# A decoder block's MLP: a written order of engines where the phases meet, first loads into early buffers, and two of four product sums per pair made by TensorE on copied banks

## The chip, the cores and the metric

The kernel runs on one core of a Trainium2 chip. The metric is the device time of one execution in microseconds (us), shown as the median of several runs. One further execution is recorded by the hardware profiler; its instruction times are the source of the rows below. PE is TensorE, DVE VectorE, ACT ScalarE, POOL GpSimd, SP SyncE (here it issues DMAs); PEld is PE's weight load.

## The reference

One layer over 1024 tokens of 1024 features in float32: a mixer half (pooling heads and state-space heads with one input and one output projection) and then an MLP half. Each half is normalised and is shifted, scaled and gated by vectors that come from a condition `c`. The change concerns the MLP half:

```python
u = rms_norm(h, g_mlp[layer]) * (1.0 + scale_f) + shift_f
f = jnp.square(jax.nn.relu(jnp.einsum('bsd,df->bsf', u, w_up[layer])))     # 1024 -> 4096
h = h + gate_f * jnp.einsum('bsf,fd->bsd', f, w_down[layer])               # 4096 -> 1024
return rms_norm(h, g_final)
```

Ahead of it stand the mixer's steps: `u = rms_norm(h) * (1 + scale_m) + shift_m`, the projection by `w_in`, windowed means, a causal convolution with silu, a chunked state-space scan, a grouped norm, and `h = h + gate_m * (y_mix @ w_out)`.

## The kernel before

**Precision.** TensorE multiplies a shortened float32 form. Each float32 operand is split into `hi` (a cast, on ACT) and `lo` (operand minus `hi`, on DVE); a product is three matmuls, hi by hi, hi by lo, lo by hi (`mm3`, line 244). So every operand needs one ACT cast and then one DVE subtraction before TensorE can use it, and PE waits for the cast and, two matmuls on, for the subtraction.

**Up-projection by seven products.** Tokens and features are halved, so u has four blocks (A11, A12 for the first 512 tokens, A21, A22 for the second), each of four 128 x 512 slices. `w_up` is taken in 16 pairs m of two 128-column groups, with blocks B11, B12, B21, B22. A Strassen-like scheme needs seven block products a pair instead of eight. Its left operands, made once, are named in `ORDER`: A11, S1 = A21 - A22, A12, E6 = S1 - A11, G3 = E6 + A12, A22, E7 = A11 - A21. Its right operands are sums of weight blocks, made per pair in `wx` or in place and split into `whl` tiles by `prep_up(m, j)`. Product j of a pair is written (m, j); a product is 4 x 3 = 12 matmuls of 512 columns. Products share PSUM banks: `KEYS` names bank a, b, c or d of the pair. `after_up(m, j)` takes results out of the banks, forms the four outputs by additions on DVE, applies squared relu (`act2`, on DVE) and writes seven combinations to DRAM (`f_d`) for the down-projection, a seven-product scheme too.

**The two meetings.** After the output projection the tokens' rows are normalised (`norm_xn`, rows `xn`), turned by PE (`turn_xn`, four 128-column transposes a bank) and scaled and shifted into u (`affine`). The first half of the tokens is done during the output projection; the second half after it. While it is made PE does six *early* products, (m, 0) and (m, 2) for the first three pairs (`NA = 3`), whose weights come from the pool of the projection's `raw`, `hi` and `lo` units. That pool is closed before the pool for the raw weights of whole pairs (`wraw`, 1 MB a load) is opened. The second meeting is that of up and down. A unit g of the down stage needs `fr` (from `f_d`) and, in the first eight units, `xs` (from `w_down`), 512 KB each (`load_dn`), and four tiles `dhi`, `dlo` in the pool `fp` (`prep_dn`). `LD = 3` units are loaded ahead and `LP = 2` are split ahead. The residual rows `hres` are read back into `tok`, whose space holds the up stage's intermediate values (`F`) until then.

**Order.** Engines run their instructions strictly in the order of their own queues. That order comes from a scheduler, except inside `pinned(...)`, where the named engines keep the written order. A tile of a pool waits until the tile that held its slot before is no longer used; the pool `fp` has 12 slots, `actp` 16.

Of the kernel before, what the change touches and what calls it, by code (L numbers as in the profile page):

```python
# [9 lines left out]
F32 = mybir.dt.float32  # L10
# [59 lines left out]
def tile_hybrid_block(  # L70
# [218 lines left out]
    um = ExitStack()  # L289
    unitm = enter(um, name="unitm", bufs=1, side="right")  # L290
    accp = enter(um, name="accp", bufs=1, side="right")
# [690 lines left out]
    F = [tok[:, 4 * i:4 * i + 4, :].rearrange("p t (a c) -> p (t a) c", c=HW) for i in range(2)]  # L982
    xn_ = {}
# [34 lines left out]

    def u2_h0(k):
# [3 lines left out]
        v = F[0][:, k, :]  # L1023
        affine(act if k % 2 == 0 else dve, v, px, k)
        dve.tensor_tensor(out=s_[:, 1, :], in0=v, in1=s_[:, 0, :].bitcast(F32), op=ALU.subtract)
        U["A11" if k < 4 else "A12"][k % 4] = s_
# [15 lines left out]
    for m in range(NA):  # L1042
        for i in range(2):
# [22 lines left out]

    ORDER = ("A11", "S1", "A12", "E6", "G3", "A22", "E7")
    MID = ("B11", "U1", "B21", "T2", "B22", "T4", "T3")
    banks, snap, wraw, wx, hl = {}, {}, {}, {}, {}

    def mm_up(m, j, w, key, first):
        b_ = banks[m, key] = bank() if first else banks[m, key]
        for k in range(4):
            a = U[ORDER[j]][k]
            whi, wlo = w[k]
            mm3(b_, whi, wlo, (a[:, 0, :], a[:, 1, :]), first and k == 0, k == 3)

    KEYS = ("a", "b", "c", "a", "b", "d", "a")
    FIRST = (True, True, True, False, False, True, False)
    LAST = (False, False, True, False, True, True, True)  # L1080
    early = [(m, i, get(1, 2)[0:4]) for m in range(NA) for i in range(2)]
    um.close()
    upst = ExitStack()
    wp = enter(upst, name="wup", bufs=1, side="right")

    def load_up(m):
        wraw[m] = wp.tile([P, KD, 2 * P], F32, name="wraw", tag="wraw", bufs=2)
# [8 lines left out]
    def prep_up(m, j):  # L1096
        r = wraw[m]
        b11, b12, b21, b22 = r[:, 0:4, 0:P], r[:, 0:4, P:2 * P], r[:, 4:8, 0:P], r[:, 4:8, P:2 * P]
        if j == 1:
            wx[m] = wp.tile([P, 4, P], F32, name="wx", tag="wx", bufs=2)  # L1100
# [8 lines left out]
        t_ = wp.tile([P, 2, 4, P], F32R, name="whl", tag="whl", bufs=4)  # L1109
        act.copy(t_[:, 0], src)  # L1110
        dve.tensor_tensor(out=t_[:, 1], in0=src, in1=t_[:, 0].bitcast(F32), op=ALU.subtract)  # L1111
        hl[m, j] = [(t_[:, 0, k, :], t_[:, 1, k, :]) for k in range(4)]

    def act2(v):
        dve.scalar_tensor_tensor(out=v, in0=v, scalar=0.0, in1=v, op0=ALU.max, op1=ALU.mult)  # L1115


    def after_up(m, j):
        f = F[m % 2]
        if j == 0:  # L1120
            s1 = f[:, 0, :]
            if m < NA:
                s1 = snap[m] = wp.tile([P, HW], F32, name="snap", tag="snap", bufs=NA)
            act.copy(s1, banks[m, "a"])
        elif j == 1:
            act.copy(f[:, 5, :], banks[m, "b"])
        elif j == 2:
            add(f[:, 0, :], banks[m, "c"], snap.get(m, f[:, 0, :]))
            act2(f[:, 0, :])
        elif j == 3:  # L1130
            act.copy(f[:, 2, :], banks[m, "a"])
        elif j == 4:
            sub(f[:, 2, :], banks[m, "b"], f[:, 2, :])
            act2(f[:, 2, :])
        elif j == 6:
            act.copy(f[:, 7, :], banks[m, "a"])  # L1136
# [10 lines left out]
    def mm_up(m, j, w):  # L1147
        key = KEYS[j]
        if FIRST[j]:
            banks[m, key] = bank()  # L1150
        for k in range(4):
            a = U[ORDER[j]][k]
            whi, wlo = w[k]
            mm3(banks[m, key], whi, wlo, (a[:, 0, :], a[:, 1, :]), FIRST[j] and k == 0, k == 3, more=not (FIRST[j] and LAST[j]))

    for n_, (m, i, w) in enumerate(early):
        mm_up(m, 2 * i, w)
        if i == 0:
            after_up(m, 0)
        r = n_ - 2 * NA + 4  # L1160
        if r >= 0:
            for k in (r, r + 4):
                affine(act, F[1][:, k, :], turn_xn(1, k), k)
    load_up(0)
    load_up(1)
    s1f = [fp.tile([P, 2, HW], F32, name="s1f", tag="a") for _ in range(2)]
    prep_up(0, 1)
    for k in range(4):
        v = s1f[k // 2][:, k % 2, :]
        sub(v, F[1][:, k, :], F[1][:, 4 + k, :])  # L1170
        U["S1"][k] = split(actp, v, "S1")
    prep_up(1, 1)
    for m in range(2):
        mm_up(m, 1, hl.pop((m, 1)))
    for k in range(4):
        v = s1f[k // 2][:, k % 2, :]
        sub(F[1][:, k, :], F[0][:, k, :], F[1][:, k, :])
        sub(F[0][:, k, :], v, F[0][:, k, :])
        U["E6"][k] = split(actp, F[0][:, k, :], "E6")
    prep_up(0, 3)  # L1180
    prep_up(1, 3)
    for m in range(2):
        mm_up(m, 3, hl.pop((m, 3)))
    for k in range(4):
        add(F[0][:, 4 + k, :], F[0][:, k, :], F[0][:, 4 + k, :])
        U["G3"][k] = split(fp, F[0][:, 4 + k, :], "G3")
    prep_up(0, 4)
    prep_up(1, 4)
    after_up(0, 2)
    after_up(0, 1)  # L1190
    after_up(0, 3)
# [240 lines left out]
```

## Time and profile before

| | |
|---|---|
| median of 3 runs (lowest to highest) | 1201.95 us (1201.36 to 1202.45) |
| profiled execution, its own time | 1201.51 us |
| its span, first to last instruction | 1199.8 us |
| mean granted TensorE clock | 0.983 |
| busy PE, DVE, ACT | 1153.1, 880.7, 520.4 us |
| end of the first meeting's transposes | 563.5 us |
| up stage at a steady pace | from about 613 us |
| first down matmul | 882.13 us |

Rows of a timeline read: start in us, length in us, engine, line, operation, output <- inputs, form, count, and in brackets the idle time of the engine before the row and who ended it. A row with a count covers consecutive instructions of one form, and its length reaches to the end of the last, whose tail overlaps the next instruction. Rows by stage give the stretch and its length, then for each engine busy us (count), then the granted clock, the DMA engines' busy share, and GB/s.

### The profile page before, as it was taken

What the parts mean: (1) busy time and instruction counts of PE and PEld (TensorE: products, weight loads), DVE (VectorE), ACT (ScalarE), POOL (GpSimd) and SP (SyncE); (2) the same over time, 40 slices, a digit from 0 to 9 for tenths busy, and PEclk for the clock granted to TensorE, in tenths of its full rate; (3) what the DMA queues carried; (4) which work ended last, traced back from release to release, by engine and by line L of the source; (5) the groups of instructions that cost most, each with busy time, mean ns of one, the idle gap of its engine ahead of it and who ended that gap; (6) DMA issues with size and microseconds to landing.
All of it is one profiled execution on the core that took longest, in us unless ns stands there. A gap on an engine that the chain in (4) does not pass through costs nothing. (4 is left out here: it accounts for less than half of the span.)

```text
span 1199.8 us, 15415 instructions
## 1 busy us (share of the span) xinstructions
PE 1153.1 (96%) x5569; PEld 950.0 (79%) x5569; DVE 880.7 (73%) x1313; ACT 520.4 (43%) x913; POOL 184.6 (15%) x208
## 2 busy tenths in 40 slices
PE   6889999999999999997989999999979999999997
PEld 5678787787899888886768888888868888888885
DVE  6978889967978646747897867777648744577984
ACT  4266575544443624527433333332324444334363
POOL 4234446515400012022000000000000000000030
PEclk9989999999999999999989999999989999999999
DMA  9831243223277637734145353444598844776732
GB/s 294 236 90 51 70 128 107 71 87 129 81 231 224 209 103 240 244 97 141 57 179 185 120 170 141 148 150 140 208 346 295 299 123 123 232 230 239 263 123 88
DMA packets 125644, 200.73 MB, mean 167 GB/s; under 512 B 8416, under 2 KB 67584, under 8 KB 123520
## 3 DMA queue, kind: packets, MB, share of 16 engines
q1 hardware_dynamic: 125072, 199.39, 50.4%
q8 instruction: 43, 0.70, 0.2%
q14 instruction: 33, 0.27, 0.1%
q10 hardware_dynamic: 240, 0.30, 0.1%
q0 software_dynamic: 256, 0.07, 0.1%
HBM read 159.81 MB, written 39.91 MB: 166 GB/s over the span
## 5 line engine op out<-in xcount | busy, mean ns | idle before, releaser
L244 PE MATMUL bank<-u,hi 128*128 128x512 f32 x560 | 186.3, 414 | 2.1 <-ACT u L252 2.0
L244 PE MATMUL bank<-dhi 128*128 128x512 f32 (+1 forms) x452 | 175.6, 390 | 7.2 <-ACT dhi L1277 6.1
L244 PE MATMUL bank<-dlo,dhi 128*128 128x512 f32 (+1 forms) x452 | 176.2, 390 | 0.6 <-DVE dlo L1278 0.6
L244 PE MATMUL bank<-dhi,dlo 128*128 128x512 f32 (+1 forms) x452 | 175.9, 389 | 0.0
L179 POOL TENSOR_TENSOR rst<-ssq,mhalf 128x1 f32<-128x1 f32 (+2 forms) x27 | 27.3, 1013 | 721.5 <-DVE ssq L178 696.4
L244 PEld LDWEIGHTS bank<-u,hi 128*128 128x128 f32 x560 | 105.3, 192 | 30.5 <-issue 5.0
L1278 DVE TENSOR_TENSOR dlo<-fr,dhi 128x1024 fp32r<-128x1024 f32 x56 | 68.5, 1222 | 81.8 <-ACT dhi L1277 81.8
L1277 ACT CAST dhi<-fr 128x1024 fp32r<-128x1024 f32 x56 | 58.6, 1047 | 155.9 <-PE bank L244 117.4
L244 PE MATMUL bank<-hi,ym 128*128 128x512 f32 x384 | 125.6, 400 | 0.0
L244 PE MATMUL bank<-u,lo 128*128 128x512 f32 x280 | 111.4, 398 | 0.0
L194 ACT CAST hi<-raw 128x512 fp32r<-128x512 f32 (+2 forms) x109 | 67.7, 631 | 87.4 <-PE bank L244 66.8
L244 PEld LDWEIGHTS bank<-dhi 128*128 128x128 f32 x452 | 85.4, 189 | 25.3 <-ACT dhi L1277 6.5
L244 PEld LDWEIGHTS bank<-dlo,dhi 128*128 128x128 f32 x452 | 85.5, 189 | 18.8 <-DVE dlo L1278 1.3
L195 DVE TENSOR_TENSOR lo<-raw,hi 128x512 fp32r<-128x512 f32 (+1 forms) x87 | 64.9, 756 | 47.8 <-ACT hi L194 46.7
L244 PEld LDWEIGHTS bank<-dhi,dlo 128*128 128x128 f32 x452 | 85.6, 189 | 17.6
L244 PE MATMUL bank<-hi,u 128*128 128x256 f32 (+1 forms) x512 | 97.7, 289 | 0.1
L244 PE MATMUL bank<-E,whl 128*128 128x512 f32 x384 | 94.8, 396 | 0.0
L244 PEld LDWEIGHTS bank<-E,whl 128*128 128x128 f32 x384 | 72.6, 189 | 17.5
L244 PEld LDWEIGHTS bank<-hi,ym 128*128 128x128 f32 x384 | 72.1, 188 | 16.2 <-issue 0.5
L244 PEld LDWEIGHTS bank<-hi,u 128*128 128x128 f32 x512 | 80.7, 190 | 1.3 <-issue 0.7
L244 PE MATMUL bank<-u,whl 128*128 128x512 f32 x312 | 77.0, 396 | 0.0
L244 PE MATMUL bank<-lo,ym 128*128 128x512 f32 x192 | 75.4, 393 | 0.0
(249 smaller groups left out, 2168.1 us busy)
## 6 DMA issues: line engine op xcount, KB each, us to landing
f_d<-tok SPq DMA_DIRECT2D x16, 1792.0 KB, 6.7
fr<-f_d SPq DMA_DIRECT2D x56, 512.0 KB, 4.1
wr<-in_w_down_dram SPq DMA_DIRECT2D x56, 512.0 KB, 5.1
raw<-in_w_ada_dram SPq DMA_DIRECT2D x64, 256.0 KB, 3.2
wraw<-in_w_up_dram SPq DMA_DIRECT2D x16, 1024.0 KB, 7.2
raw<-in_w_in_dram SPq DMA_DIRECT2D x48, 256.0 KB, 2.9
raw<-in_w_out_dram SPq DMA_DIRECT2D x48, 256.0 KB, 2.8
tok<-in_x_dram SPq DMA_DIRECT2D x16, 512.0 KB, 6.3
```

The costliest lines, as they stand in the source:

```text
L179: pool.tensor_tensor(out=rst[:, a:b], in0=m, in1=mhalf[:, :b - a], op=ALU.pow)
L194: act.copy(hi[:, :n], raw[:, :n])
L195: (pool if ring.get("pool_lo") else dve).tensor_tensor(out=lo[:, :n], in0=raw[:, :n], in1=hi[:, :n].bitcast(F32), op=ALU.subtract)
L244: pe.matmul(ps, lhsT=st_, rhs=mv, start=first and i == 0, stop=last and i == 2, skip_group_check=more)
L1277: act.copy(hi, src)
L1278: dve.tensor_tensor(out=lo, in0=src, in1=hi.bitcast(F32), op=ALU.subtract)
```

## The change

1. Left operands. S1 is made directly: ACT scales the turned A22 slice with a bias of the two shifts' difference (`dsh`), DVE scales the turned A21 slice and subtracts it, so S1 needs no separate u values. The shift is added to A22 later, in place on ACT. E6, G3, E7 and A22 are formed and split two slices at a time (1024 columns, `two`, `hi2`, `lo2`). `LONG` and `SHORT` name the slots of `F` where slices that live longer or shorter stand.
2. Order. The early units are all A11 first and A12 after. Then one `pinned` block writes ACT's, DVE's and PE's order from the first early product to (1, 5): three A11 products, the transposes and the S1 slices between the A12 products, S products for pairs 0 to 2, and so on. `prep_up` is split into `prep_hi` and `prep_lo`. From pair 4 on products run in the order 0, 1, 3, 2, 6, 4, 5.
3. Buffers. Pair 0's `wraw` and some `whl` tiles come from a new pool on the other side (`wupl`, every third pair) or from `lp`, so that they need not wait for the unit pool. The first three units' `fr` and all `xs` go to `actp`, and the first three units' loads are issued by POOL's queue during pair 15, with the first two `prep_dn` between pair 15's products.
4. Sums. `onward` copies bank a to a new bank on ACT (after product 0 to c, after 6 to d), and products 2 and 5 accumulate on the copy, in place of two DVE additions a pair. Relu and square of these two outputs move to ACT. The transposes clear a bank's accumulate state only with the first of four.

The diff's core:

```diff
     def turn_xn(h, k):
         px = bank()
         for i in range(4):
-            turn(px[:, i * P:(i + 1) * P], xn_[4 * h + i][:, k * P:(k + 1) * P])
+            pe.matmul(px[:, i * P:(i + 1) * P], lhsT=xn_[4 * h + i][:, k * P:(k + 1) * P], rhs=ident,
+                      is_transpose=True, start=i == 0, stop=i == 3, skip_group_check=True)
...
+    early = [get(1, 2)[0:4] for _ in range(2 * NA)]
+    am.close()
+    wlst = ExitStack()
+    wl = enter(wlst, name="wupl", bufs=1)
...
     def load_up(m):
-        wraw[m] = wp.tile([P, KD, 2 * P], F32, name="wraw", tag="wraw", bufs=2)
+        wraw[m] = (upp["r"] if m % 3 else wl).tile([P, KD, 2 * P], F32, name="wraw", tag="wraw", bufs=2 if m % 3 else 1)
...
+    def act2_bank(v, b_):
+        act.activation(out=v, in_=b_, func=AF.Relu)
+        act.activation(out=v, in_=v, func=AF.Square)
...
+    def onward(m, key):
+        banks[m, key] = bank()
+        act.copy(banks[m, key], banks[m, "a"])
...
     def after_up(m, j):
         f = F[m % 2]
         if j == 0:
-            s1 = f[:, 0, :]
-            if m < NA:
-                s1 = snap[m] = wp.tile([P, HW], F32, name="snap", tag="snap", bufs=NA)
-            act.copy(s1, banks[m, "a"])
+            onward(m, "c")
...
         elif j == 2:
-            add(f[:, 0, :], banks[m, "c"], snap.get(m, f[:, 0, :]))
-            act2(f[:, 0, :])
+            act2_bank(f[:, 0, :], banks[m, "c"])
...
         elif j == 6:
-            act.copy(f[:, 7, :], banks[m, "a"])
-            sub(f[:, 5, :], f[:, 5, :], f[:, 7, :])
-            add(f[:, 7, :], banks[m, "d"], f[:, 7, :])
-            act2(f[:, 5, :])
-            act2(f[:, 7, :])
+            onward(m, "d")
+            sub(f[:, 5, :], f[:, 5, :], banks[m, "a"])
+            (act2 if m > 1 else act2_on_act)(f[:, 5, :])
+        else:
+            act2_bank(f[:, 7, :], banks[m, "d"])
...
+    load_up(0)
+    with pinned((act, dve, pe)):
+        for m in range(NA):
+            mm_up(m, 0, early[m])
+            if m == 0:
+                prep_up(0, 1)
+        for m in range(NA):
+            after_up(m, 0)
         for k in range(4):
...
+            px = turn_xn(1, k + 4)
+            v = F[1][:, LONG[k], :]
+            act.activation(out=v, in_=px, func=AF.Identity, scale=sc_f[:, k + 4:k + 5], bias=dsh[:, k:k + 1])
+            px = turn_xn(1, k)
+            o = F[1][:, SHORT[k], :]
+            dve.scalar_tensor_tensor(out=o, in0=px, scalar=sc_f[:, k:k + 1], in1=v, op0=ALU.mult, op1=ALU.subtract)
+            s_ = actp.tile([P, 2, HW], F32R, name="S1", tag="a")
+            act.copy(s_[:, 0, :], o)
+            sub(s_[:, 1, :], o, s_[:, 0, :].bitcast(F32))
+            U["S1"][k] = (s_[:, 0, :], s_[:, 1, :])
+            if k < 3:
+                mm_up(k, 2, early[NA + k])
...
     def load_dn(g):
         p, u = units[g]
-        fr[g] = dp.tile([P, 2, HW], F32, name="fr", tag="fr", bufs=4)
-        sp.dma_start(out=fr[g], in_=f_d[u][:, :, PROD[p], :])
+        if g < LD:
+            fr[g] = actp.tile([P, 2, HW], F32, name="fr0", tag="a")
+        else:
+            fr[g] = dpp["d"].tile([P, 2, HW], F32, name="fr", tag="fr", bufs=4)
+        q = pool if g < LD else sp
+        q.dma_start(out=fr[g], in_=f_d[u][:, :, PROD[p], :])
...
+        if m == 15:
+            if j == 3:
+                for g in range(LD):
+                    load_dn(g)
+            elif j in (6, 4):
+                prep_dn(j == 4)
```

What this does to the queues, at the places where PE waits. First, DVE where the second half of u is made, before the change. (`s1f`, `S`, `G`, `E`: left operands and their lo parts; `wx` and `whl`: weight sum and its lo part.)

```order
L1094 TENSOR_TENSOR s1f<-tok 128x512
L1014 TENSOR_TENSOR G_5799<-tok,G_5799 128x512
L1094 TENSOR_TENSOR tok<-tok 128x512
L1014 TENSOR_TENSOR S_5704<-s1f,S_5704 128x512
L1091 TENSOR_TENSOR wx<-wraw 128x512
L1014 TENSOR_TENSOR E_5740<-tok,E_5740 128x512
L1014 TENSOR_TENSOR E_5745<-tok,E_5745 128x512
L1111 TENSOR_TENSOR whl<-wx,whl 128x512
```

And DVE at the same place after the change:

```order
L1101 TENSOR_TENSOR wx<-wraw 128x512
L178 TENSOR_SCALAR ssq<-ssq 128x1
L1141 TENSOR_TENSOR whl<-wx,whl 128x512
L1211 SCALAR_TENSOR_TENSOR tok<-bank,sc_f,tok 128x512
L1104 TENSOR_TENSOR S_5613<-tok,S_5613 128x512
...
L1104 TENSOR_TENSOR S_5694<-tok,S_5694 128x512
L1101 TENSOR_TENSOR wx<-wraw 128x512
L1104 TENSOR_TENSOR tok<-tok 128x2x512
L1141 TENSOR_TENSOR whl<-wx,whl 128x512
```

The first pair's weight sum and its split moved ahead of all four S1 slices (and ahead of the last row's `ssq`); the G and E work between the S1 slices moved behind them.

Second, ACT where up meets down, before the change:

```order
L1110 CAST whl<-wraw 128x512
L1131 COPY tok<-bank 128x512
L1136 COPY tok<-bank 128x512
L1277 CAST dhi<-fr 128x1024
L1277 CAST dhi<-xs 128x1024
```

And after it (`fr_7698` and `fr_7702` are the first two units' `fr` tiles):

```order
L1174 COPY tok<-bank 128x512
L1178 COPY tok<-bank 128x512
L1152 ACTIVATE tok<-bank 128x512
L1153 ACTIVATE tok<-tok 128x512
L1356 CAST dhi<-fr_7698 128x1024
L1356 CAST dhi<-xs 128x1024
L1166 COPY bank<-bank 128x512
L1356 CAST dhi<-fr_7702 128x1024
```

The first down unit's two casts now stand ahead of pair 15's copy from bank a to bank d (L1166), on which product (15, 5) accumulates; before, they stood behind the last bank of up.

Third, SP's queue at the same meeting, before and then after (`f_d_84` is the last pairs' result, `hres_69` to `hres_76` the eight rows of residuals, `fr<-f_d_80` unit 3's load):

```order
L1312 DMA tok<-hres_70 128x1024
L1255 DMA fr<-f_d_77 128x2x512
L1255 DMA fr<-f_d_78 128x2x512
L1255 DMA fr<-f_d_79 128x2x512
L1145 DMA f_d_84<-tok 128x3584
L1312 DMA tok<-hres_71 128x1024
...
L1312 DMA tok<-hres_76 128x1024
L1255 DMA fr<-f_d_80 128x2x512
```

```order
L1378 DMA gfin<-in_g_final_dram 128x1024
L1408 DMA tok<-hres_70 128x1024
L1408 DMA tok<-hres_71 128x1024
L1408 DMA tok<-hres_72 128x1024
L1334 DMA fr<-f_d_80 128x2x512
L1334 DMA fr<-f_d_81 128x2x512
L1334 DMA fr<-f_d_82 128x2x512
L1192 DMA f_d_84<-tok 128x3584
L1321 DMA xs<-in_w_down_dram 128x2x512
L1334 DMA fr<-f_d_83 128x2x512
L1408 DMA tok<-hres_73 128x1024
```

Units 3 to 5 moved ahead of the last `f_d` write and of the second half of the residual rows; the loads of units 0 to 2 left this queue for POOL's.

More of the change, by code (lines that the diff above doesn't have):

```diff
@@ L1017, in tile_hybrid_block, with two, hi2, lo2 @@
     U = {n: [None] * 4 for n in ("A11", "A12", "A22", "S1", "E6", "G3", "E7")}
+    def two(f, slots, i):
+        a, b = slots[2 * i], slots[2 * i + 1]
+        return F[f][:, a:b + 1:b - a, :]
+    def hi2(p, name, src):
+        hi = p.tile([P, 2, HW], F32R, name=name, tag="a")
+        act.copy(hi, src)
+        return hi, p.tile([P, 2, HW], F32R, name=name, tag="a"), src, name
+    def lo2(i, t_):
+        hi, lo, src, name = t_
+        dve.tensor_tensor(out=lo, in0=src, in1=hi.bitcast(F32), op=ALU.subtract)
+        for k in range(2):
+            U[name][2 * i + k] = (hi[:, k, :], lo[:, k, :])
     def u2_h0(k):
@@ L1067, in tile_hybrid_block @@
     ORDER = ("A11", "S1", "A12", "E6", "G3", "A22", "E7")
[L1068 to L1076, printed above, removed]
-    KEYS = ("a", "b", "c", "a", "b", "d", "a")
[L1079 to L1084, printed above, removed]
+    KEYS = ("a", "b", "c", "a", "b", "d", "a")
+    banks, wraw, wx, hl = {}, {}, {}, {}
+    early = [get(1, 2)[0:4] for _ in range(2 * NA)]
+    am.close()
+    wlst = ExitStack()
+    wl = enter(wlst, name="wupl", bufs=1)
+    dsh = const.tile([P, 4], F32, name="dsh")
+    dve.tensor_tensor(out=dsh, in0=sh_f[:, 4:8], in1=sh_f[:, 0:4], op=ALU.subtract)
+    upp = {}
     def load_up(m):
-        wraw[m] = wp.tile([P, KD, 2 * P], F32, name="wraw", tag="wraw", bufs=2)
+        wraw[m] = (upp["r"] if m % 3 else wl).tile([P, KD, 2 * P], F32, name="wraw", tag="wraw", bufs=2 if m % 3 else 1)
         sp.dma_start(out=wraw[m], in_=wup_r[:, :, 2 * m * P:(2 * m + 2) * P])
@@ L1145, in after_up @@
             sp.dma_start(out=f_d[m // 2][:, m % 2, :, :], in_=f[:, 0:7, :])
[L1147 to L1150, printed above, removed]
-        for k in range(4):
[L1152 to L1179, printed above, removed]
@@ L1210, in tile_hybrid_block @@
+    steps = [(3, 0), (3, 1), (3, 2), (2, 6), (3, 3), (2, 4), (2, 5), (3, 6), (3, 4), (3, 5)]
+    for m in range(4, 16):
+        steps += [(m, j) for j in (0, 1, 3, 2, 6, 4, 5)]
     done = 0
@@ L1214, in ahead @@
         while done < min(n, len(steps)):
[L1215 to L1218 removed]
+            prep_up(*steps[done])
             done += 1
[L1221 to L1239 removed]
+    ahead(1)
+    after_up(0, 5)
+    ahead(2)
+    after_up(1, 5)
+    after_up(2, 1)
+    after_up(2, 3)
+    after_up(2, 2)
     PROD = (0, 1, 3, 4, 6, 2, 5)
@@ L1280, in prep_dn @@
         fw[g] = made
+    for n_, (m, j) in enumerate(steps):
+        ahead(n_ + 3)
+        if (n_ == 2 or j == 0) and m + 1 < 16 and m + 1 not in wraw:
+            load_up(m + 1)
+        up(m, j)
+        if m == 15:
[4 more added lines that the diff above has]
+                prep_dn(j == 4)
+        after_up(m, j)
+    upst.close()
+    wlst.close()
+    dpp["d"] = enter(ctx, name="down", bufs=1, side="right")
+    gfin = lp.tile([P, D], F32, name="gfin", tag="gm")
+    sp.dma_start(out=gfin, in_=g_final.unsqueeze(0).broadcast_to([P, D]))
     def mm_dn(ps, g, kk, i, first, last, c0=0, c1=HW):
```

192 lines of the change are left out of this document (122 added, 70 removed).

## Prediction

> **What bounds the kernel now.** I read, in this order: the page's busy shares and slices, the table of busy time by stage, and the timelines of PE, DVE, ACT and SP around the two stages that fall out of line.
>
> ```profile
> PE 1153.1 (96%) x5569; PEld 950.0 (79%) x5569; DVE 880.7 (73%) x1313; ACT 520.4 (43%) x913; POOL 184.6 (15%) x208
> PEclk9989999999999999999989999999989999999999
> ...
> 550.00:600.00 50.00, 43.73 (x193) 34.85 (x192) 40.36 (x66) 27.79 (x48) 0.55 (x1) 0.93 0.28 87
> 600.00:650.00 50.00, 46.79 (x186) 36.45 (x185) 43.46 (x72) 16.45 (x29) 0.00 (x0) 0.93 0.46 169
> 650.00:700.00 50.00, 50.00 (x216) 40.28 (x215) 35.65 (x56) 15.24 (x27) 0.00 (x0) 1.00 0.49 165
> 850.00:900.00 50.00, 43.33 (x174) 34.27 (x173) 26.71 (x37) 14.02 (x19) 0.00 (x0) 0.90 0.79 296
> 900.00:950.00 50.00, 50.00 (x222) 41.39 (x222) 40.81 (x36) 22.15 (x25) 0.00 (x0) 1.00 0.90 309
> ```
>
> PE is the bound. In the steady stretch 650:700 it is never idle, at full granted clock. Time can be won only where PE waits or its clock falls: where normalisation meets the up-projection (550 to 650) and where up meets down (850 to 900). First meeting, PE alone (start, length, what, idle ahead of it):
>
> ```profile
> 562.74 1.03 PE L138 MATMUL bank<-ident,xn 128*128 128x128 f32 x8
> 569.47 8.55 PE L244 MATMUL bank<-S,whl 128*128 128x512 f32 x24 [5.70 <-ACT whl L1110]
> 577.85 5.76 PE L244 MATMUL bank<-E,whl 128*128 128x512 f32 x24
> 583.45 5.76 PE L244 MATMUL bank<-G,whl 128*128 128x512 f32 x24
> 589.05 5.76 PE L244 MATMUL bank<-A,whl 128*128 128x512 f32 x24
> 594.65 5.76 PE L244 MATMUL bank<-E,whl 128*128 128x512 f32 x24
> 602.33 1.22 PE L244 MATMUL bank<-S,whl 128*128 128x512 f32 x2 [1.91 <-ACT whl L1110]
> 604.03 4.64 PE L244 MATMUL bank<-S,whl 128*128 128x512 f32 x10 [0.48 <-DVE whl L1111]
> 608.46 3.28 PE L244 MATMUL bank<-E,whl 128*128 128x512 f32 x12
> 612.56 0.73 PE L244 MATMUL bank<-A,whl 128*128 128x512 f32 x2 [0.82 <-ACT whl L1110]
> 613.13 2.98 PE L244 MATMUL bank<-G,whl 128*128 128x512 f32 x12
> ```
>
> At full pace 24 matmuls take 589.05 - 583.45 = 5.60 us (0.2333 each, 2.80 a product of 12). The first 24 after the idle 5.70 took 577.85 - 569.47 = 8.38: a fallen clock, 2.78 us more. The same pace of about 0.44 follows 602.33, after a gap of 602.33 - 600.25 = 2.08. From the end of the transposes (562.74 + 0.79) to 613.13 are 49.6 us for 24x5 + 2 + 10 + 12 + 2 = 146 matmuls, which cost 34.1: **15.5 us lost**.
>
> Second meeting:
>
> ```profile
> 873.09 2.96 PE L244 MATMUL bank<-E,whl 128*128 128x512 f32 x12
> 882.13 1.65 PE L244 MATMUL bank<-dhi 128*128 128x512 f32 x3 [6.09 <-ACT dhi L1277]
> 884.37 0.79 PE L244 MATMUL bank<-dlo,dhi 128*128 128x512 f32 x1 [0.59 <-DVE dlo L1278]
> 889.16 0.40 PE L244 MATMUL bank<-dhi,dlo 128*128 128x512 f32 x1
> 873.42 1.91 SPq L1255 DMA_DIRECT2D fr<-f_d  x3
> ```
>
> Up ends at 873.09 + 2.80 = 875.89; full pace returns at 889.16. The 14 matmuls between would cost 14 x 50/222 = 3.2, so 13.3 - 3.2 = **10.1 us lost**. The first fr transfer was issued at 873.42, 2.5 us before up ended. Together 25.6 us: without them the profiled 1201.5 (span 1199.8 and 1.7 around it) would be 1175.9. The median of the runs, 1201.95, lies 0.4 above the profiled run.
>
> **The change, part by part.** The number of matmuls stays. Prices, from rows of before:
>
> ```profile
> 601.48 1.89 DVE L1094 TENSOR_TENSOR tok<-tok 128x512 f32<-128x512 f32 x3
> 884.23 1.22 DVE L1278 TENSOR_TENSOR dlo<-fr,dhi 128x1024 fp32r<-128x1024 f32 x1
> 885.37 1.22 DVE L1278 TENSOR_TENSOR dlo<-xs,dhi 128x1024 fp32r<-128x1024 f32 x1
> 856.48 0.59 ACT L1136 COPY tok<-bank 128x512 f32<-128x512 f32 x1 [2.18 <-PE bank L244]
> 856.97 0.62 ACT L1110 CAST whl<-wx 128x512 fp32r<-128x512 f32 x1
> 552.44 1.45 ACT L1006 ACTIVATE tok<-bank,sh_f,sc_f 128x512 f32<-128x512 f32 x2 [0.42 <-PE bank L138]
> ```
>
> Back to back, DVE takes 0.60 for 512 columns (three in 1.89, the last's tail in it) and 1.14 for 1024; ACT takes 0.49 to 0.52, 0.72 with scale and bias.
>
> *Product sums on copied banks.* Per pair DVE loses four operations (2.4 us of each 19.6 us, the seven products) and ACT gains four (about 2.1). The stage's DVE share falls from 0.71 to about 0.59 and ACT's rises from 0.30 to 0.41: both hidden, so no gain either. New is that PE waits for an ACT copy twice a pair: the first has two products (5.6 us), the second one product (2.80) of cover. A copy of 0.59 behind two other ACT operations is done in 1.7. I take zero; uncovered, it costs the excess over 2.80, fourteen times.
>
> *S1 made between the early products.*
>
> ```profile
> 550.88 1.15 ACT L992 ACTIVATE xn<-tok,rst 128x1024 f32<-128x1024 f32 x1 [0.85 <-POOL rst L179]
> 552.08 0.77 PE L138 MATMUL bank<-ident,xn 128*128 128x128 f32 x5 [0.57 <-ACT xn L992]
> 568.08 0.68 DVE L1091 TENSOR_TENSOR wx<-wraw 128x512 f32<-128x512 f32 x1
> 568.80 0.62 ACT L1110 CAST whl<-wx 128x512 fp32r<-128x512 f32 x1 [0.26 <-DVE wx L1091]
> ```
>
> In before DVE reaches wx only at 568.08, behind the S1, E6 and G3 work; that ended the wait at 569.47. Now wx and its cast stand ahead of all that, and the weights' load is issued ahead of the six early units. wx pushes the last row's rst, hence xn, by one DVE operation: +0.5 us on the idle 0.57. Each of four steps then needs 0.72 + 0.60 + 0.52 + 0.60 = 2.4 us on ACT and DVE, under the 2.80 + 0.79 that PE has between two pairs of transposes. After the last pair PE works 9 matmuls (2.1 us) before the fourth slice: 0.4 of wait. So S starts about 6 us earlier, with the clock up.
>
> *The written order after it.* DVE runs S1's fourth lo, wx of pair 1, half of E6 (1.14), pair 1's lo. PE needs the cast (0.60 + 0.62 after S1's lo, which comes 0.7 before PE is free: 0.5 of wait) and, two matmuls on, that lo (2.4 after: 0.75). The same for pair 2: 1.14 + 2 x 0.60 + 1.14 + 0.60 = 4.1 us of DVE against 2.80 of PE: 1.3. E6, G3 and E7 products then find their operands. Before (0,5) DVE runs a subtraction, two A22 lo's, wx and a lo after (0,6) ends: 0.60 + 2.28 + 0.60 + 0.60 = 4.1 against the 2.80 of (1,6), and PE's order holds one matmul of pair 3, whose raw weights go into pair 0's tile:
>
> ```profile
> wraw<-in_w_up_dram SPq DMA_DIRECT2D x16, 1024.0 KB, 7.2
> xs<-in_w_down_dram SPq DMA_DIRECT2D x8, 512.0 KB, 8.0
> 13.25 0.74 POOL L448 DMA_DIRECT2D adaa<-in_conv_w_dram  x1
> ```
>
> That load can go out only after pair 0's last sum, some 5 us before (0,5), and lands 7.2 later; with the cast, 2.2 us of wait in two or three pieces. Bounds for this group: 2.5 (waits overlap) to 8 (each twice as long). Taken: 0.5 + 0.4 + 1.25 + 1.3 + 2.2 = 5.7.
>
> *The clock.* Rows show a gap of 0.82 without slow matmuls behind it and one of 2.08 with them. The 2.2 us about (0,5) lie within some 3 us, nearer to the second: I count one fall, 2.8. Bounds: none, or two (5.6). The Trainium skill, page "TensorE: Matmul & The Clock Gate", section "Why this matters for your kernels", allows idle gaps up to about 3 us before the clock drops; by it no fall, and the time would be 1182. Here the 2.08 row disagrees with it.
>
> *First loads.* Three fr and three xs move to POOL's queue and to act slots that the A11 and S1 products free. Pair 15 uses them as its first two products, 19.6 to 14 us before up ends; at 0.74 an issue and 8.0 to land the first two arrive 9 us before the end. Their casts stand 7 and 5.6 us before it (slots freed inside (15,6)). First casts and lo's, 2 x 0.95 + 1.14, end before PE is free: loss 10.1 to about 0.3. The later loads (fr 3 to 5) now stand ahead of the last f_d write and of hres 4 to 7 on SP.
>
> *Sum:* 1201.5 - 15.5 - 10.1 + 5.7 + 2.8 + 0.3 = 1184.7; **predicted 1185 us**.
>
> **Rivals.**
>
> A, *transfers become the bound as down starts.* From 19 us before up's end to unit 7 (33 after) go: 14 pieces of fr and xs of 512 KB, hres and gfin (4.7 MB), two f_d writes (3.7 MB), two later pieces (1 MB): 16.8 MB in 52 us, 323 GB/s, against 309 seen in 900:950 and 296 in 850:900. For: nearly nothing is spare. Against: that row had PE full. Price: 4.5% of 52 us is 2.3; with a fall of the clock (2.8) and a second late unit as long, 1190 to 1193.
>
> B, *POOL's loads come late.* ACT's order has both first casts ahead of the copy that product (15,5) waits for, so a late load also stops up and the f_d write. For: no 512 KB load on that queue in this trace. Against: issued 18.9 us before up's end and wanted 7 before it, the first may take 11.9 us to land. Price: the second meeting's gain, 1195. The Trainium skill, page "SBUF — State Buffer", section "Who interferes with whom", has loads issued by GpSimd starve while VectorE holds the port pair the two share, which speaks for this rival; no row here shows it.
>
> C, *slower:* the copies sit on PE's path. The mechanism is ACT's strict order in pairs 2 to 15; it decides once a copy ends 4.0 us after its product (2.80 covered, 1.2 x 14 = the 16.8 gained). At 5 us it costs 14 x 2.2 = 31: 1216. Against: ACT is idle ahead of its bank reads (2.18 above).
>
> D, *the meetings only swap waits:* the clock falls twice more and the gain of the first meeting halves: 1192. E, *no change:* every wait taken away comes back in another place, which needs all of the above at once.
>
> **How the numbers follow.** Forecast 1180 to 1190: 0.62. A 0.13, B 0.07, D 0.10, C 0.04, E 0.04. The low end is no fall of the clock and the small waits at their lower bound: 1201.5 - 25.6 + 2.5 + 0.3 = 1178.7. The high end takes in A, D and B: 1196. Within 0.2% (2.4 us) is what this measurement can't tell from no change. Faster: all but C and E, 0.92; same 0.04; slower 0.04.
>
> **What would show it.** S products start near 564 with no idle over 0.7 ahead of them; granted clock 1.0 in 550:600; between 565 and 598 PE idle of 4 to 7 us in pieces under 1.5; no PE idle over 1 us where up meets down; POOL loads landing before ACT's first dhi. Wrong would be: PE idle released by ACT's bank copies in 650:850 (C), idle released by DMA within 40 us of down's start (A), or half-pace matmuls after pieces under 1 us.

## The result

| | before | after |
|---|---|---|
| median (lowest to highest) | 1201.65 us (1200.35 to 1202.45) | 1181.11 us (1180.30 to 1181.33) |
| profiled execution, its span | 1201.51, 1199.8 us | 1180.30, 1178.6 us |
| busy PE, DVE, ACT | 1153.1, 880.7, 520.4 us | 1144.6, 838.3, 558.1 us |

The ratio after to before is 0.9829, with a 95% interval of 0.9812 to 0.9846: faster by 1.7%, against a forecast of 1185 us (1179 to 1196).

From the page of the kernel after, the row of the granted clock by slices:

```profile
PEclk9989999999999999999999999999999999999999
```

Of the three digits 8 of the kernel before, the two at the meetings are gone. By stage (the stretch, then busy us and count of PE, PEld, DVE, ACT and POOL, granted clock, DMA share, GB/s):

```profile
550.00:600.00 50.00, 45.22 (x204) 34.85 (x203) 39.07 (x52) 35.80 (x56) 0.55 (x1) 1.00 0.23 74
600.00:650.00 50.00, 50.00 (x218) 40.66 (x217) 40.17 (x67) 26.56 (x49) 0.00 (x0) 1.00 0.65 231
650.00:700.00 50.00, 50.00 (x218) 40.65 (x217) 31.96 (x49) 21.42 (x39) 0.00 (x0) 1.00 0.43 163
850.00:900.00 50.00, 50.00 (x221) 41.19 (x220) 26.34 (x28) 21.57 (x25) 1.73 (x3) 1.00 1.00 377
```

Both meetings run at full clock, and PE is idle only in the first. The third row holds something the prediction had no term for: 218 matmuls in 50 us, where the kernel before did 216.

The first meeting, PE alone:

```profile
564.32 1.04 PE L1002 MATMUL bank<-ident,xn 128*128 128x128 f32 x8
565.83 3.01 PE L244 MATMUL bank<-S,whl 128*128 128x512 f32 x12 [0.48 <-ACT tok L1208]
569.25 0.73 PE L244 MATMUL bank<-S,whl 128*128 128x512 f32 x2 [0.41 <-ACT whl L1136]
570.34 2.56 PE L244 MATMUL bank<-S,whl 128*128 128x512 f32 x10 [0.35 <-DVE whl L1141]
573.57 3.44 PE L244 MATMUL bank<-S,whl 128*128 128x512 f32 x12 [0.67 <-ACT tok L1152]
...
596.29 0.40 PE L244 MATMUL bank<-A,whl 128*128 128x512 f32 x1
597.24 0.49 PE L244 MATMUL bank<-A,whl 128*128 128x512 f32 x1 [0.55 <-DVE A L1032]
598.45 0.50 PE L244 MATMUL bank<-u,whl 128*128 128x512 f32 x1 [0.71 <-ACT whl L1136]
599.58 5.40 PE L244 MATMUL bank<-A,whl 128*128 128x512 f32 x22 [0.63 <-DVE whl L1141]
604.81 2.66 PE L244 MATMUL bank<-u,whl 128*128 128x512 f32 x11
```

The lengths hold a tail that overlaps the next row, so gaps are taken from start to start, with 0.2333 us for each matmul. Ahead of S: 565.83 - 564.32 - 0.79 = 0.72. In the second S product: 569.25 - 565.83 - 2.80 = 0.62, and 570.34 - 569.25 - 0.47 = 0.62. Ahead of the third: 573.57 - 570.34 - 2.33 = 0.90. Around (0,5): 0.72, 0.98 and 0.90, together 2.6. The sum is 5.5 us, and the 22 matmuls behind the last gap take 604.81 - 599.58 = 5.23, 0.238 each: the clock did not fall, and the granted clock of this stretch is 1.00.

The second meeting: PE's rows, POOL's first issue, ACT's first casts and the first wait of ACT, then the landing times of POOL's loads (last number, us):

```profile
862.53 2.96 PE L244 MATMUL bank<-A,whl 128*128 128x512 f32 x12
865.33 0.39 PE L244 MATMUL bank<-dhi 128*128 128x512 f32 x1
...
847.30 0.80 POOL L1334 DMA_DIRECT2D fr<-f_d  x1 [294.97 <-ACT whl L1136]
...
858.38 1.03 ACT L1356 CAST dhi<-fr 128x1024 fp32r<-128x1024 f32 x1
...
875.28 1.05 ACT L1356 CAST dhi<-fr 128x1024 fp32r<-128x1024 f32 x1 [7.54 <-DMA fr<-f_d]
...
fr<-f_d POOLq DMA_DIRECT2D x3, 512.0 KB, 7.6
xs<-in_w_down_dram POOLq DMA_DIRECT2D x3, 512.0 KB, 12.5
```

The last up product takes its 2.80 us and the first down product follows at once. ACT's first cast stands 7 us before the end of up and waits for no load.

**Where the 21.2 us of the profiled runs (1201.5 - 1180.3) went.** First meeting: 15.5 lost before, 5.5 now, and 0.3 more ahead of it (below): 9.7. Second: 10.1 lost before, nothing now. That leaves 1.4 us, which come from neither meeting; they are the subject of the first experiments.

### The profile page after: what moved, and what is told of

Read it like the earlier page. It is cut to its first block, busy times and chain, and to the rows that moved or that the text cites. A ratio compares the mean times of both kernels' runs of the same rounds, so it can differ in the third digit from the quotient of the medians.

```text
span 1178.6 us, 15348 instructions
## 1 busy us (share of the span) xinstructions
PE 1144.6 (97%) x5569; PEld 944.7 (80%) x5569; DVE 838.3 (71%) x1232; ACT 558.1 (47%) x977; POOL 189.9 (16%) x214
## 4 chain that ended last, share of the span: by engine, by line
PE 86%; DVE 7%; DMA 2%; ACT 2%; issue 1%; POOL 1%; SPq 1%; POOLq 0%; ACTq 0%; DVEq 0%
PE bank L244 78%; DVE cv L541 3%; PE bank L719 2%; PE bank L138 1%; PE bank L723 1%; PE bank L716 1%; DMA raw<-in_w_in_dram 1%; DVE adaa L266 1%; DMA adaw<-in_w_ada_dram 1%; PE bank L795 1%; PE bank L1002 1%; DMA tok<-in_x_dram 1%; DVE cv L552 1%; DVE lo L195 0%; POOL tok L952 0%
```

## Experiment 1: two products in six run faster, and the output projection slower

PE's rows in the steady stretch of the kernel after:

```profile
668.37 2.96 PE L244 MATMUL bank<-A,whl 128*128 128x512 f32 x12
671.17 2.89 PE L244 MATMUL bank<-u,whl 128*128 128x512 f32 x12
673.90 2.89 PE L244 MATMUL bank<-S,whl 128*128 128x512 f32 x12
```

A takes 671.17 - 668.37 = 2.80, u takes 2.73. Over many pairs two products in a row of every six are fast, whichever operand they have. Six is the length of the rotation of weight tiles in the changed code: two come from pools of the left stack (`wl`, `lp`), four from the right (`wup`). In the kernel before all came from the right. At the same time the 576 matmuls on `ym` became slower, though the diff doesn't touch them. First and last of them, in the kernel before:

```profile
399.86 0.48 PE L244 MATMUL bank<-hi,ym 128*128 128x512 f32 x1
...
542.39 0.39 PE L244 MATMUL bank<-hi,ym 128*128 128x512 f32 x1
```

and in the kernel after:

```profile
399.71 0.48 PE L244 MATMUL bank<-hi,ym 128*128 128x512 f32 x1
...
543.57 0.40 PE L244 MATMUL bank<-hi,ym 128*128 128x512 f32 x1
```

That is 142.53 us before and 143.86 after. What did change is the place of everything: the new constant `dsh` moved the left stack up by 32 bytes a partition.

The first kernel makes that constant longer and changes nothing else:

```diff
-    dsh = const.tile([P, 4], F32, name="dsh")
+    dsh = const.tile([P, 12], F32, name="dsh")[:, 0:4]
```

> The changed kernel with one constant tile 32 bytes per partition longer, so that every tile of the left stack (the products' moving operands, the ym tiles, two of the six weight tiles in rotation) lies 32 bytes higher, while the right stack (the other four weight tiles, the raw units of the output projection) stays. No instruction is added or moved. In the changed kernel two products of every six take 2.73 us and four 2.80, whatever the operand; the two are those whose weight tile lies in the left stack. Theory RELATIVE: PE's pace hangs on the distance between the weights' address and the moving operand's, and is best when it is a multiple of 4096 bytes; with the shift it is one for all six weight tiles. Then all 106 products take 2.73, 70 of them 0.07 faster: 4.9 us less; the 576 matmuls on ym, which took 143.9 us instead of 142.5 after the change's own 32-byte shift, come back to 142.5 or less: 1174 to 1175 us. Theory ABSOLUTE: 64-byte alignment of each address counts; then all six weight tiles and all operands are at 32 modulo 64 as in the kernel before, every product takes 2.80, the 36 fast ones lose 2.5 us and the ym part regains 1.4: about 1182. Theory REGION: only the place in the upper memory counts; two of six stay fast, 1180.

Measured: 1175.57 us (1175.17 to 1175.62), ratio to before 0.9789 (0.9774 to 0.9803). Every product takes 2.72. The steady stretch, and the first and last matmul on `ym`:

```profile
650.00:700.00 50.00, 50.00 (x223) 41.40 (x222) 33.33 (x52) 21.61 (x39) 0.00 (x0) 1.00 0.46 174
...
400.07 0.48 PE L244 MATMUL bank<-hi,ym 128*128 128x512 f32 x1
...
542.46 0.39 PE L244 MATMUL bank<-hi,ym 128*128 128x512 f32 x1
```

223 matmuls instead of 218, and 142.39 us instead of 143.86. The four right weight tiles are at the same addresses as before and have become fast, since the operands moved: so neither the upper region nor a 64-byte alignment of each address decides: ABSOLUTE and REGION are out. What decides is how weights and moving operand lie to each other.

The same on the kernel before, one unused constant of 64 bytes, which gives the right tiles the same distance:

```diff
     const = enter(ctx, name="const", bufs=1)
+    const.tile([P, 16], F32, name="pad")
```

> The kernel before with one unused constant tile of 64 bytes per partition, so that the left stack lies 64 bytes higher and the distance from every weight tile of the up-projection to its moving operand is a multiple of 4096 bytes; no instruction differs. Theory RELATIVE (which the shift of the changed kernel by 32 bytes bore out): the 106 products go from 2.80 to 2.72 us; some 90 of them are back to back, 7 us: about 1193.5 against 1200.5, and the steady stretch shows 222 matmuls in 50 us instead of 216. Rival: the pace depends on something else that the change brought, such as the tiles with two high or two low slices; then 1200.5.

Measured: 1192.86 us (1191.57 to 1195.51), ratio 0.9934 (0.9918 to 0.9950), every product 2.72. So the effect has nothing to do with the change's operand layout: 64 bytes of nothing are worth 8 us to the kernel before.

Three kernels tried how fine the distance matters, by spacing the four right tiles wider:

```diff
-            t_ = upp["r"].tile([P, D], F32R, name="whl", tag="whl", bufs=4)
+            t_ = upp["r"].tile([P, D + 8], F32R, name="whl", tag="whl", bufs=4)[:, :D]
```

> The changed kernel with the four weight tiles of the right stack spaced by 4128 instead of 4096 bytes. Modulo 4096 their distances to the moving operands become -96, -64, -32 and 0 (they were all +32); the two left weight tiles stay at 0. Theory RELATIVE with 4096: of the six tiles in rotation three are fast (2.73 or less) and three slow (2.80); the gain over the changed kernel is 18 products of 0.07, 1.2 us: 1179.5. RELATIVE with 64: the tile at -64 is fast too, 1178. ABSOLUTE: addresses at 0 modulo 64 are fast, which are the two left ones, the second (-64) and the fourth (0) of the right: 1178 as well, so it is told from RELATIVE with 64 by the shift of the left stack alone. REGION: 1181, no change.

Measured: 1180.21 us (1178.58 to 1182.27). By the place in the rotation the products take 2.72 and 2.73 (left tiles), then 2.80, 2.77, 2.79 and 2.75. By the addresses in the built program these four tiles lie at -96, 0, -32 and -64. So the tile at distance 0 takes 2.77 and not 2.72, right behind a slow product: its first eight matmuls are slow, its last four take 0.227 each, the best pace.

The other two add 32 and 16 elements instead of 8, on top of the 32-byte shift:

> The changed kernel with the left stack 32 bytes higher and the four right weight tiles spaced by 4224 bytes: their distances to the moving operands become -512, -384, -256 and -128 modulo 4096, the two left tiles stay at 0. The slices inside a tile lie 512 bytes apart and all ran alike, so a rule can't go by more than 512. If it goes by 128 or less, all six tiles take 2.72 us a product; if by 512, three of six fall back towards 2.80 (the one at -512 and the two left ones stay); if by 256, two do.

> The same with the four right weight tiles spaced by 4160 bytes: distances -256, -192, -128 and -64. If the pace goes by multiples of 128, the tiles at -256 and -128 take 2.72 and those at -192 and -64 more (2.77 was seen at -64, 2.80 at +64 and at 32 from a multiple); if by 64 with something else behind the 2.77, all take 2.72.

Measured, a single run each: 1178.32 and 1179.30 us. With the addresses from the built programs and the starts from the traces, the products of all these kernels sort by the distance of their weight tile:

| weights minus moving operand, bytes (modulo 4096) | 12 matmuls, us |
|---|---|
| 0 | 2.72 (2.72 to 2.77 right behind a slow product) |
| -256, -512 | 2.72, 2.73 (2.76 at -256 right behind a slow product) |
| -64 | 2.75 |
| +64, +32, -32, -96, -128, -192, -384 | 2.79 to 2.80 |

A product right behind a slow one needs up to eight matmuls until it runs at 0.227. So of the rules named above the one by 256 bytes fits the products: distances of 0, -256 and -512 are best, and -128 and -384 are not. The matmuls on `ym` don't follow it: they took 142.5 us at 64 and 192 bytes modulo 256, 142.4 at 0 and 128, and 143.9 at 96 and 224. Why the distance sets the pace stays open.

For the result this means: 36 of the 106 products gained 0.07, 2.6 us; the matmuls on `ym` lost 1.3. The net 1.3 is nearly all of the 1.4 left over above.

## Experiment 2: the product sums

Pairs 4 to 15 go back to sums on DVE:

```diff
...
+        if m >= 4 and j == 0:
+            act.copy(f[:, 0, :], banks[m, "a"])
+        elif m >= 4 and j == 2:
+            add(f[:, 0, :], banks[m, "c"], f[:, 0, :])
+            act2(f[:, 0, :])
...
+            if m >= 4:
+                add(f[:, 7, :], banks[m, "d"], f[:, 7, :])
+                act2(f[:, 7, :])
```

> The changed kernel with the two product sums by TensorE on copied banks undone in pairs 4 to 15: the third product and the sixth start in a fresh bank, ACT copies the first sum to the f tile as before the change, DVE adds the two and does relu and square, four operations of DVE more a pair and four of ACT fewer. The prediction's theory: both are hidden behind PE, no change, 1180 to 1181, with DVE's share of the steady stretch going from 0.64 to about 0.75 and ACT's from 0.43 to about 0.33. Rival: the copies are what made the steady stretch of the changed kernel faster (218 matmuls in 50 us, 216 before), because fewer DVE reads of banks and tiles disturb PE; then the stretch falls back to 216 and the time rises by about 2 us, to 1183. Second rival: DVE is now so full that f arrives late at the next pair's reuse; then PE idles behind DVE, 1 us or more a pair, 1193 or over.

Measured: 1179.75 us (1178.81 to 1183.20), ratio 0.9830 (0.9808 to 0.9851) against 0.9829 for the whole change. Its steady stretch:

```profile
650.00:700.00 50.00, 50.00 (x218) 40.59 (x217) 38.34 (x60) 16.51 (x29) 0.00 (x0) 1.00 0.47 174
```

DVE goes from 31.96 to 38.34 us, ACT from 21.42 to 16.51, PE's 218 stay. The sums on copied banks are worth nothing here in these twelve pairs, as forecast, and the rival that they made PE faster falls.

## Experiment 3: the second meeting, put back; and the queue

The first kernel gives the first loads their old tiles, SP's queue and their place behind the loop:

```diff
-        if g < LD:
-            fr[g] = actp.tile([P, 2, HW], F32, name="fr0", tag="a")
-        else:
-            fr[g] = dpp["d"].tile([P, 2, HW], F32, name="fr", tag="fr", bufs=4)
-        q = pool if g < LD else sp
+        fr[g] = dpp["d"].tile([P, 2, HW], F32, name="fr", tag="fr", bufs=4)
+        q = sp
...
```

> The changed kernel with the second meeting alone put back: the first three f loads go into tiles of the down pool again, which come free when the up-projection ends, on SP's queue behind the loop, and the first two casts stand behind the loop too; everything else, the order of the first meeting included, is as changed. The prediction's theory: the first loads' places were all of the second meeting, so its 10.1 us come back (the changed kernel has no idle there): 1180.5 + 10.1 = 1190.6, with the first down product waiting some 6 us on ACT's cast of f and half-pace matmuls behind it. Rival: part of the old loss came from the order of the last pair's products, which stays changed; then less than 7 us come back, 1185 to 1187.

Measured: 1190.36 us (1188.92 to 1191.39), ratio 0.9909 (0.9896 to 0.9923): 9.2 us come back. PE where up meets down:

```profile
861.28 2.96 PE L244 MATMUL bank<-A,whl 128*128 128x512 f32 x12
871.71 1.65 PE L244 MATMUL bank<-dhi 128*128 128x512 f32 x3 [7.46 <-ACT dhi L1353]
```

Up ends at 864.08 and PE stands still for 7.6 us, with slow matmuls behind it. That is the old picture, so the places of the first loads were the second meeting.

The second kernel keeps places and time and changes only the queue:

```diff
-        q = pool if g < LD else sp
+        q = sp
```

> The changed kernel with the first three f loads and first three weight loads of the down-projection issued on SP's queue instead of POOL's, at the same place in the program and into the same tiles. Theory: the places and the early issue did the work, and the queue is indifferent, since SP has only two f writes and two raw loads near that time: 1180 to 1181, no PE idle where up meets down. Rival: POOL's queue was needed, because the loads stand on SP behind a write that waits for the last sums of the pair ahead; then the first cast on ACT waits and stops up's copies too, 3 us or more: 1184 or over.

Measured: 1185.20 us (1183.78 to 1185.64), ratio 0.9869 (0.9852 to 0.9885): 4.1 us slower than the change. The theory was wrong, though not as the rival had it. Up meets down without idle; the wait comes 24 us later, ahead of the fifth down unit. SP's issues, then ACT's cast and PE's row:

```profile
870.54 0.33 SPq L1192 DMA_DIRECT2D f_d<-tok  x1
...
877.35 1.75 SPq L1408 DMA_DIRECT2D tok<-hres  x4
879.15 0.43 SPq L1321 DMA_DIRECT2D xs<-in_w_down_dram  x1
...
888.04 1.04 ACT L1356 CAST dhi<-xs 128x1024 fp32r<-128x1024 f32 x1 [6.88 <-DMA xs<-in_w_down_dram]
...
889.14 0.74 PE L244 MATMUL bank<-dhi 128*128 128x512 f32 x2 [2.76 <-ACT dhi L1356]
```

With the first six loads on SP the scheduler puts the fifth unit's `xs` load behind the last f write, which waits for the last sums, and behind four residual rows. It is issued at 879.15, its cast starts at 888.04, and PE waits 2.76. The granted clock falls behind that wait (891.17 to 894.58); from 885.99 to 894.61 PE does 14 matmuls, 3.2 us of work, so 5.4 us are lost, about what the profiled runs differ by (1185.47 against 1180.30). In the kernel after, SP had issued the fourth and fifth units' `xs` loads at 850.98 and 851.68, while POOL issued the first ones. So the first loads themselves were in time on either queue, and POOL's mattered by what then stood ahead of the later loads on SP's.

## Experiment 4: the written order of the first meeting

The same program text without the pins:

```diff
-    with pinned((act, dve, pe)):
+    with ExitStack():
         for m in range(NA):
             mm_up(m, 0, early[m])
```

> The changed kernel without the written order: the instructions of the first meeting are issued in the same program order, but ACT, DVE and PE are no longer held to it, and the scheduler places them. In its order DVE makes the first two E6 operations between the S1 steps and puts wx of pair 1 and 2 behind the E6 rests. Theory of the prediction: the written order is what lets S start near 564 and pairs 1 and 2 follow; without it S products start two to three DVE operations later (1.2 to 2.3 us) and the products of pairs 1 and 2 wait about 2 us more each, some 4 to 7 us together and likely a fall of the clock: 1185 to 1188. Rival: most of the first meeting's gain comes from what is done (S1 made in two operations between the early products, wx early), not from the pins: 1180 to 1182.

Measured: 1189.80 us (1189.44 to 1191.46), ratio 0.9908 (0.9895 to 0.9922): 8.7 us slower, more than either theory. PE's waits, then ACT's last `xn` and its bank copies:

```profile
555.78 0.62 PE L244 MATMUL bank<-u,hi 128*128 128x512 f32 x1 [2.13 <-ACT bank L1166]
...
575.42 0.74 PE L244 MATMUL bank<-S,whl 128*128 128x512 f32 x2 [2.08 <-ACT whl L1136]
577.22 5.49 PE L244 MATMUL bank<-S,whl 128*128 128x512 f32 x12 [1.06 <-DVE whl L1141]
...
554.09 1.15 ACT L993 ACTIVATE xn<-tok,rst 128x1024 f32<-128x1024 f32 x1 [0.51 <-POOL rst L179]
555.15 1.55 ACT L1166 COPY bank<-bank 128x512 f32<-128x512 f32 x3
```

I had looked only at DVE's order. The scheduler also puts the three `onward` copies on ACT behind the last `xn`, and PE's A12 products accumulate on those copies: that is the wait at 555.78. The two waits in the second S product follow from DVE's order as expected, and the 12 matmuls behind them take 5.28 us instead of 2.80: the clock fell. A further wait that neither theory has lies behind the block: at 623.51 PE waits 2.02 us for a bank copy of ACT, which itself waited for pair 0's f write, and the clock falls once more (624.28 to 627.69); these two cost 3.7 us. So without the pins 8.7 us are lost, nearly as much as the first meeting's whole gain of 9.7. Whether the pins would be worth as much without S1's two operations or without the early raw weights was not tested.

## Experiment 5: how long may PE idle before the clock falls

Before the first product of five pairs PE waits for a chain of ACT operations that starts when PE closes a bank:

```diff
...
+        if j == 0 and m in GAPS:
+            t_ = hl[m, j][0][0][:, 0:1]
+            act.copy(gj, banks[m - 1, "d"])
+            for _ in range(GAPS[m]):
+                act.copy(gj, gj)
+            act.activation(out=gz, in_=gj[:, 0:1], func=AF.Copy, scale=0.0)
+            act.activation(out=t_, in_=t_.bitcast(F32), func=AF.Identity, bias=gz)
         up(m, j)
```

> The changed kernel with PE made to wait before the first product of pairs 5, 7, 9, 11 and 13: a chain of ACT operations reads the bank that PE has just closed, is 0, 1, 2, 4 or 7 copies longer, and then touches the weights that PE needs next. By the changed kernel's copies of 0.57 us, the gaps should be about 1.5, 2.1, 2.7, 3.8 and 5.5 us. This measures after what single idle time the granted clock falls, and what the fall costs. By my prediction's rule (the gap of 2.08 us in the kernel before had matmuls of 0.44 us behind it) the gaps from 2.1 on are followed by a fall of 2.8 us each, the first isn't: the idle of 15.6 us and four falls of 2.8 make about 1207. By the Trainium skill's rule in the page TensorE: Matmul & The Clock Gate (gaps up to about 3 us are free of it) only the last two are: about 1201.

Measured, a single run: 1205.76 us. The small constant `gz` moves the left stack by 32 bytes too, so the base is the 1175.6 of the shifted kernel, and the total tells nothing between the two rules; the rows do. The first two gaps:

```profile
647.67 2.88 PE L244 MATMUL bank<-A,whl 128*128 128x512 f32 x12
653.04 3.01 PE L244 MATMUL bank<-u,whl 128*128 128x512 f32 x12 [2.48 <-ACT whl L1374]
655.89 2.88 PE L244 MATMUL bank<-S,whl 128*128 128x512 f32 x12
...
688.53 2.88 PE L244 MATMUL bank<-A,whl 128*128 128x512 f32 x12
694.55 4.32 PE L244 MATMUL bank<-u,whl 128*128 128x512 f32 x12 [3.15 <-ACT whl L1374]
698.67 1.63 PE L244 MATMUL bank<-S,whl 128*128 128x512 f32 x5
```

The first gap is 653.04 - 647.67 - 2.72 = 2.65 us, longer than planned, and the product behind it takes 2.85, 0.13 too long: no fall. The second is 3.30, and the product behind it takes 4.12, with 0.34 more in the next: 1.7 us lost. The other three, of 3.95, 5.26 and 7.21 us, cost 2.65, 1.9 and 2.2. So by these five my rule is wrong, and the other fits.

The cluster of three gaps around (0,5) speaks against both. Nine profiled kernels have it, with the same order. With a sum of 2.55 to 2.59 us (four kernels, the change itself among them) the 22 matmuls behind it took 5.23 to 5.24. With 2.67, 2.70, 2.77 and 2.97 they took 6.70 to 6.78: a fall that costs 1.5. With 2.99 they took 5.12, no fall. So it is not the length alone that decides.

The traces show what does, since they record when the granted clock was at half. In each of the thirteen traces the falls begin and end on a grid of 3.41 us, and last one, two or three of its steps (but for the last, which the trace's end cuts off); where the grid lies differs from run to run. In the kernel with the gaps they begin at 695.96, 736.92, 781.29 and 829.08, which are 12, 13 and 14 steps apart. PE's idle time, taken from start to start, was then added up in each step between 400 and 1150 us in which the clock was full. Of these 2825 steps 19 hold 2.08 us of idle time or more, and a fall begins at the end of each; the others hold 1.98 or less, and none has a fall behind it. Two steps next to the cluster, the change's and then the shifted kernel's with the step behind it (busy us and count of PE, granted clock, DMA share, GB/s; matmuls' tails count as busy here):

```profile
595.05:598.46 3.41, 2.15 (x10) 1.00 0.61 214
...
595.85:599.26 3.41, 1.77 (x5) 1.00 0.10 28
599.26:602.67 3.41, 3.41 (x9) 0.50 0.89 286
```

The end of a step at 598.46 cuts the change's 2.59 us into 1.69 and 0.90; of the shifted kernel's 2.97 us, 2.27 lie in one step. The first of the five gaps is cut into 1.20 and 1.45. So the edge lies near 2 us of idle time within one step, and whether a cluster or a single gap of 2 to 4 us brings a fall depends on where the grid lies in that run. A fall costs half of the part of it in which PE works: 1.7, 2.7, 1.9 and 2.2 us for the second to the fifth gap, as measured. The Trainium skill, page "TensorE: Matmul & The Clock Gate", section "Part 1: The HAM clock gate (the "warmup" mystery)", describes a window of about 3.4 us that runs freely; the grid in these traces agrees with it.

## Experiment 6: a version that beats both

The waits around (0,5) come from DVE's written order: two subtractions that only free banks, one of them waiting for ACT, stand ahead of the low parts that PE needs. The order is mended on top of the 32-byte shift:

```diff
         after_up(0, 4)
         prep_hi(0, 5)
-        after_up(1, 4)
-        after_up(0, 6)
         lo2(0, made[0])
-        up(1, 6)
         lo2(1, made[1])
-        prep_hi(1, 5)
         prep_lo(0, 5)
-        after_up(1, 6)
+        after_up(0, 6)
+        prep_hi(1, 5)
+        after_up(1, 4)
         prep_lo(1, 5)
+        up(1, 6)
+        after_up(1, 6)
```

> The changed kernel with the left stack 32 bytes higher and the written order around the fifth product of pair 0 mended: DVE makes the two low parts of A22 and of that product's weights ahead of the subtractions that only free banks, and ACT copies the sum onward before it squares pair 1's. In the shifted kernel PE lost 2.98 us in three waits there (two behind DVE, one behind the cast that waits for pair 3's raw weights) and 1.5 us in a fall of the clock behind them. Theory: those waits go and nothing else is late: 1175.6 - 3.0 - 1.5 = 1171 (1172.5 in runs in which the clock would not have fallen). Rival: the raw weights of pair 3, which load into pair 0's tile, set the pace, and the wait comes back one product later: 1174 to 1176.

Measured: 1172.55 us (1171.07 to 1173.05), ratio 0.9758 (0.9745 to 0.9771): 3.0 us below the shifted kernel, of the 3.0 to 4.5 expected, and 8.6 below the change. The last gap of the cluster and the 22 slow matmuls behind it, in the shifted kernel:

```profile
598.49 6.89 PE L244 MATMUL bank<-A,whl 128*128 128x512 f32 x22 [0.60 <-DVE whl L1141]
```

and the place in the mended one:

```profile
595.65 2.88 PE L244 MATMUL bank<-A,whl 128*128 128x512 f32 x12
598.60 0.73 PE L244 MATMUL bank<-u,whl 128*128 128x512 f32 x2
599.61 0.50 PE L244 MATMUL bank<-u,whl 128*128 128x512 f32 x1 [0.28 <-DVE whl L1141]
599.94 2.91 PE L244 MATMUL bank<-A,whl 128*128 128x512 f32 x12
```

The first A product runs through. Of 2.97 us of gaps 0.9 are left (598.60 - 595.65 - 2.72 = 0.23, then 0.55 and 0.10), at pair 3's first matmuls, and no slow matmuls follow. The rival, that the wait for pair 3's raw weights comes back whole, doesn't hold.

## Why the prediction was right, and where it was not

**What bounds the kernel:** right. From 200 us on PE was full in both kernels outside the two meetings (50.00 us of each 50), and the whole gain but 1.4 us came from them.

**First meeting, the small waits:** 5.7 forecast, 5.5 + 0.3 measured, and term by term: ahead of S 0.4 forecast, 0.72 measured; (1,1) 1.25 and 1.24; (2,1) 1.3 and 0.90; around (0,5) 2.2 and 2.6, with the releasers that were named (DVE, then the cast behind the raw weights, then DVE). The later `xn` was 0.5 in the forecast; ACT's row of it came 1.5 later, of which 1.2 is the slower `ym` part ahead of it, so 0.3. S started at 565.83 and not near 564 for the same reason and for the 0.72.

**The clock:** the term of 2.8 us for one fall behind the (0,5) gaps was wrong in this run, in its place and in its size. The reading under it holds: in the kernel before, the clock fell at 602.35, the end of the gap of 2.08, all of which lay in one step of the grid. But the change's 2.6 us were cut by the end of a step, and nothing fell. That was luck: the cluster's 2.55 to 2.99 us brought a fall in four of nine kernels, at 1.5 us, so a term of about half of that was the right size. The 2.78 came from a fall of two steps (568.21 to 575.04) behind the long wait for S. The Trainium skill's rule that I set aside, in the page "TensorE: Matmul & The Clock Gate", section "Why this matters for your kernels" (about 3 us are free), gave the better time, 1182. It is no safer as a rule here: falls came behind single gaps of 2.08 us (before, 602.35) and 2.30 us (without the pins, 555.78).

**Second meeting:** 0.3 forecast, nothing lost; putting it back cost 9.2 us, against the 10.1 that I read from the rows.

**The sums:** zero forecast, zero measured in pairs 4 to 15. DVE's share of the steady stretch came to 0.64, where 0.59 was forecast, ACT's to 0.43 against 0.41; neither cost PE anything.

**What had no term:** the weight tiles' place, +2.6 us of gain in up and 1.3 us of loss in the projection. The prediction took "the number of matmuls stays" to mean that their pace stays. The sum after the fact is 1201.5 - 15.5 - 10.1 + 5.8 - 1.3 = 1180.4, against 1180.3 profiled; the forecast of 1184.7 was too high by the clock's 2.8, the places' 1.3 and the 0.3.

**The rivals:** A (transfers the bound) didn't happen, but was near. The DMA engines moved 377 GB/s, all of them busy (850:900), more than the 309 that I had as the most seen, and ACT waited 7.5 us for a later unit's `fr` load with PE covered; with the first loads on SP's queue, a later `xs` load made PE wait 2.8. B: POOL's `xs` loads took 12.5 us to land where I had 8.0 from SP's rows; a first cast wanted 11.1 us after the first issue still found its `fr`, which took 7.6. By the Trainium skill, page "SBUF — State Buffer", section "Who interferes with whom", such loads starve while VectorE holds the port pair that it shares with GpSimd. No run here shows that: SP's own five `xs` loads in the same run took a median of 11.6 us to land, and all eight 9.9 when SP issued them, so crowded DMA engines may be the whole cause. C and D: the bank copies end nothing on PE's path in the steady stretch, and the waits did not swap. But without the pins bank copies did hold PE (555.78), so C's mechanism is real, and in the first meeting the written order kept it away.

## What to carry to other kernels

Add up PE's idle time in each step of the clock's 3.41 us grid, and not gap by gap: 1.98 us or less in a step cost no fall here, 2.08 or more always brought one, and those measured one by one cost 1.5 to 2.8 us. Where the grid lies changes from run to run, so small waits that stand close together and add up to 2 us are worth mending even in a run that shows no fall. When a change adds even one small constant or moves a pool, compare the pace of matmuls that it does not touch, product by product: 32 bytes a partition moved this kernel by 5 us. When a written order is the change, look at every engine's order, not the busiest's alone.

## What was not expected of the hardware

- The same 12 matmuls took 2.72 to 2.80 us by the distance in memory between weights and moving operand, at full clock with no idle time; distances of 0, -256 and -512 bytes were best. 576 other matmuls took 142.4 us or 143.9 us by a shift of 32 bytes.
- Between 400 and 1150 us of the thirteen traces the granted clock fell only at the ends of steps of a 3.41 us grid, and only where PE had idled 2.08 us or more within the step; three short waits brought a fall as one long one did.
- The DMA engines reached 377 GB/s over 50 us beside a PE that was never idle.
